# Compressed k and v projections of a sparse-attention layer: one pass over the contraction in place of two

## The chip, the core and the metric

One core of a Trainium2 chip runs the whole kernel. The metric is the device time of one execution in microseconds; lower is better. Several executions are timed and their median counts. Another execution is taken with a profiler, and the rows below come from that one.

## What is computed

One decoder layer on 256 positions of width 2048, in float32, with native sparse attention: three branches (compressed blocks, selected blocks, sliding window) with keys and values of their own. What matters here is the first step, the projections of the compressed branch and the compression behind them:

```python
h = x @ w_in                                   # x: 256 x 2048
q, kc, vc, ks, vs, kw, vw, gl, z = split_cols(h, NSA_SPLITS)   # kc, vc: 512 columns each
...
def nsa_compress(kv, pe, w1, w2):              # for kc and for vc
    blocks = kv[:, idx] + pe[None, None, :, None, :]           # 15 blocks of 32 positions, stride 16
    hid = silu(einsum('bnlgd,lde->bnge', blocks, w1))
    return einsum('bnge,ef->bngf', hid, w2)
```

Behind it come the other projections, the attention of 16 heads in four groups, a gate, the output projection and a layer norm.

## The kernel before

The contraction of 2048 is cut into 16 chunks of 128 (`KC`). Every float32 operand is split into an upper and a lower part: ScalarE writes the upper half (`whi`, `xs`; L66), VectorE subtracts to get the lower half (`wlo`; L67). `mm_w` (L102 to L104) then runs a pair of matmuls for one weight block of 128 columns and one chunk: the upper weights against both halves of x (512 columns), and the lower weights against the upper half of x (256 columns). The sum of both stands in one PSUM bank; `join` (L106 to L110) adds its two halves with one ScalarE and one VectorE instruction into one of two buffers.

The front of the program (L125 to L160) runs over "k", then over "v". Each has four column groups, so four PSUM banks: for k `proj` three times and `o`, for v `sc` twice and `tr` twice; these eight are all there are. In the k pass each step loads x (`load_x`, L78; four buffers `kt`) and the k weights (`big`, eight buffers, L134 to L137): one chunk at a time for the first eight, then two. The x halves stay in SBUF for all later projections. The v pass loads its weights in four loads of four chunks (`load_w`, L60, three buffers `wraw`). The weight splits go to `whi` and `wlo`, four buffers each. After its pass, each of k and v is joined and split into `hi` and `lo` of compressed layout (L154 to L159).

`compress_hidden` (L178) multiplies these with `w1`, 48 matmuls for each of k and v. Its weights come as two loads (`wraw`), split in four pieces (`whi`, `wlo`), one per twelve matmuls. It runs for k first; then come the table of the position bias (L232, L233) and the projections of group 0 (`proj_t`, L252), with the compression of v behind the first of them.

All loads are issued by SP in one queue. The program names the instructions in an order, and a scheduler sets the order on each engine from it, by a plan of the time at which buffers and operands come free. An instruction whose operands are there can go ahead of one named earlier.

Of the kernel before, what the change touches and what calls it, by code (L numbers as in the profile page):

```python
# [11 lines left out]
F32 = mybir.dt.float32  # L12
F32R = mybir.dt.float32r
# [3 lines left out]
P = 128  # L17
# [3 lines left out]
NG = 4  # L21
HPG = 4
KC = DM // P
NCMP = 15
CLEN = 32
CSTRIDE = 16
# [5 lines left out]
LU = 384  # L32
KTW = 4 * P + 16
CM = NG * 16 + 2
HALVES = ((0, 256), (256, 512))
HALF_TO = 1
CUTS_K = (0, 1, 2, 3, 4, 5, 6, 7, 8, 10, 12, 14, 16)


@with_exitstack  # L40
def nsa_layer(ctx, tc, A, out):
    nc = tc.nc
# [4 lines left out]
    wp = ctx.enter_context(tc.tile_pool(name="wp", bufs=1))  # L47
    sb = ctx.enter_context(tc.tile_pool(name="sb", bufs=1))
# [5 lines left out]
    def bank(tag):  # L54
        return ps.tile([P, 512], F32, name=tag, bufs=BUFS[tag])
# [4 lines left out]
    def load_w(src, k, n):  # L60
        raw = wp.tile([P, k, n], F32, name="wraw", bufs=3)
        nc.sync.dma_start(raw, src)
        return raw

    def split_into(hi, lo, src):
        act.activation(hi, src, AF.Copy)  # L66
        dve.tensor_tensor(lo, src, hi.bitcast(F32), op=ALU.subtract)  # L67

    def split_w(raw, k0, k1):
        n = raw.shape[2]  # L70
        hi = wp.tile([P, k1 - k0, n], F32R, name="whi", bufs=4)
        lo = wp.tile([P, k1 - k0, n], F32R, name="wlo", bufs=4)
        split_into(hi, lo, raw[:, k0:k1, :])
        return hi, lo
# [3 lines left out]
    def load_x(k0, k1):  # L78
        raw = sb.tile([P, KTW], F32, name="kt", bufs=4)[:, :(k1 - k0) * SEQ]
        raw = raw.rearrange("p (k s) -> p k s", s=SEQ)  # L80
        nc.sync.dma_start(raw, A["xT"][:, k0:k1, :])
        c, o = divmod(k0, 4)
        if o == 0:
            X2[c] = [xp.tile([P, 2, 2 * SEQ], F32R, name="xs") for _ in range(2)]
        t = X2[c][o // 2][:, o % 2:o % 2 + k1 - k0, :]
        hi, lo = t[:, :, :SEQ], t[:, :, SEQ:]
        if k0 == 0:
            dve.tensor_copy(hi, raw)
            dve.tensor_tensor(lo, raw, hi.bitcast(F32), op=ALU.subtract)
        else:  # L90
            split_into(hi, lo, raw)

    def xk(k):
        return X2[k // 4][k % 4 // 2][:, k % 2, :]

    def xh(k):
        return xk(k)[:, :SEQ]
# [4 lines left out]
    def mm_w(acc, hi, lo, k):  # L102
        pe.matmul(acc, hi, xk(k), start=(k == 0), stop=False)  # L103
        pe.matmul(acc[:, :SEQ], lo, xh(k), start=False, stop=(k == KC - 1))  # L104

    def join(acc, scale=1.0):  # L106
        t = sb.tile([P, SEQ], F32, name="join", bufs=2)
        act.activation(t, acc[:, SEQ:], AF.Copy, scale=scale)  # L108
        dve.scalar_tensor_tensor(t, acc[:, :SEQ], scale, t, op0=ALU.mult, op1=ALU.add)  # L109
        return t  # L110
# [4 lines left out]
    def load_small():  # L115
        for n, shape in (("peT_k", [P, CLEN]), ("peT_v", [P, CLEN]), ("w2_k", [P, P]), ("w2_v", [P, P]),
                         ("rel", [2 * CSTRIDE, NH]), ("gmask", [P, 3 * HPG])):
            t = const.tile(shape, F32, name=n)
            nc.sync.dma_start(t, A[n])
            small[n] = t  # L120
# [1 line left out]
    ident = const.tile([P, P], F32, name="ident")  # L122
    make_identity(nc, ident)

    tags = {"k": ["proj", "proj", "proj", "o"], "v": ["sc", "sc", "tr", "tr"]}  # L125
    kvc = {}
    cuts = {"k": CUTS_K, "v": (0, 4, 8, 12, 16)}
    for which, name in enumerate("kv"):
        accs = [bank(t) for t in tags[name]]
        for k0, k1 in zip(cuts[name], cuts[name][1:]):  # L130
            src = A["wkvc"][which, :, k0:k1, :]
            if name == "k":
                load_x(k0, k1)
                raw = sb.tile([P, CSTRIDE * CM], F32, name="big", bufs=8)[:, :(k1 - k0) * 512]  # L134
                raw = raw.rearrange("p (k n) -> p k n", n=512)
                for n0, n1 in HALVES if k0 < HALF_TO else ((0, 512),):
                    nc.sync.dma_start(raw[:, :, n0:n1], src[:, :, n0:n1])  # L137
            else:
                raw = load_w(src, k1 - k0, 4 * P)
            if name == "k" and k1 == KC:  # L140
                load_small()
            for ka in range(k0, k1, 2):
                kb = min(ka + 2, k1)
                if name == "k" and k0 < HALF_TO:
                    hi, lo = (wp.tile([P, 1, 512], F32R, name=n, bufs=4) for n in ("whi", "wlo"))
                    for n0, n1 in HALVES:
                        split_into(hi[:, :, n0:n1], lo[:, :, n0:n1], raw[:, :, n0:n1])
                else:
                    hi, lo = split_w(raw, ka - k0, kb - k0)
                for g in range(NG):  # L150
                    cs = slice(g * P, (g + 1) * P)
                    for k in range(ka, kb):
                        mm_w(accs[g], hi[:, k - ka, cs], lo[:, k - ka, cs], k)
        hi, lo = (sb.tile([P, CSTRIDE, CM], F32R, name="big", bufs=8) for _ in range(2))  # L154
        for g in range(NG):
            view = [t[:, :, g * 16:(g + 1) * 16].rearrange("p l n -> p n l") for t in (hi, lo)]
            split_into(*view, join(accs[g]).rearrange("p (n l) -> p n l", l=CSTRIDE))
        view = [t[:, :, 64:66].rearrange("p l a -> p a l") for t in (hi, lo)]
        split_into(*view, small["peT_" + name].rearrange("p (a l) -> p a l", a=2))  # L159
        kvc[name] = hi, lo  # L160
# [10 lines left out]
    for i in range(2):  # L171
        t = const.tile([P, HPG, 64], F32R, name=f"pcs{i}")
# [329 lines left out]
    def split_held(raw, half, hi):  # L502
        lo = sb.tile([P, 2, 512], F32R, name="bias", bufs=2)
        split_into(hi[:, 2 * half:2 * half + 2], lo, raw[:, 2 * half:2 * half + 2, :])
        return hi[:, 2 * half:2 * half + 2], lo

    for c in range(4):
# [4 lines left out]
        for hq in range(4):  # L512
            raw = load_w(A["wo"][c, hq], 4, 512)
            if c == 0 and hq == 3:
                load_res()
            for half in range(2):
                if c == 3 and hq == 1:
                    if half == 0:
                        held_hi = sb.tile([P, HPG, 512], F32R, name="t1", bufs=1)
                    w = split_held(raw, half, held_hi)  # L520
                else:
                    w = split_w(raw, 2 * half, 2 * half + 2)
# [19 lines left out]
        n0, n1 = Norm(0), Norm(1)  # L542
# [37 lines left out]
def _layout(inputs):  # L580
    f = lambda n: np.asarray(inputs[n])
    x = np.ascontiguousarray(f("x").reshape(SEQ, DM))
    w = f("w_in_a")

    def rows(a):
        return a.reshape(-1, P, a.shape[-1]).transpose(1, 0, 2)

    arr = {"x": x}
    arr["xT"] = rows(x.T)
    arr["wkvc"] = np.stack([rows(w[:, o:o + 512]) for o in (2048, 2560)])  # L590
    wt = []
    for g in range(NG):
        cols = [3072 + g * P, 4096 + g * P]
        cols += [(HPG * g + h) * P for h in range(HPG)]
        cols += [5168 + (HPG * g + h) * P for h in range(HPG)]
        wt += [rows(w[:, c:c + P]) for c in cols]
    arr["wt"] = np.stack(wt)
    wv = []
    for g in range(NG):
        panel = np.concatenate([w[:, 3584 + g * P:3584 + (g + 1) * P], w[:, 4608 + g * P:4608 + (g + 1) * P],  # L600
                                w[:, 5120 + 12 * g:5120 + 12 * (g + 1)]], axis=1)
        wv.append(np.stack([rows(panel[h * 1024:(h + 1) * 1024]) for h in range(2)]))
    arr["wv"] = np.stack(wv)
    wo = f("w_out_a")
    arr["wo"] = np.stack([np.stack([rows(wo[q * 512:(q + 1) * 512, c * 512:(c + 1) * 512]) for q in range(4)])
                          for c in range(4)])
    for n in "kv":
        arr["peT_" + n] = f("cmp_pe_" + n).T
        arr["w1_" + n] = f("cmp_w1_" + n).reshape(2, 16, P, P).transpose(2, 1, 0, 3).reshape(P, 16, 2 * P)
        arr["w2_" + n] = f("cmp_w2_" + n)  # L610
    arr["rel"] = f("rel_bias")
    arr["ln_g"] = f("ln_g_a")
    arr["ln_b"] = f("ln_b_a")
    oh = np.zeros((33, LU), np.float32)
    m = np.arange(LU)
    oh[_bucket(np.maximum(m - 127, 0)), m] = 1.0
    oh[:, :127] = 0.0
    oh[32, :127] = 1.0
    arr["onehot"] = oh
    cs = np.zeros((CM, 2, P), np.float32)  # L620
    for g in range(NG):
        for n in range(NCMP):
            j = 16 * g + n
            cs[j, 0, j] = cs[64, 0, j] = cs[j + 1, 1, j] = cs[65, 1, j] = 1.0
    arr["csel"] = cs
    gm = np.ones((P, HPG, 3), np.float32)
    gm[:31, :, 0] = 0.0
    arr["gmask"] = gm.reshape(P, 12)
    return {k: np.ascontiguousarray(v) for k, v in arr.items()}
# [15 lines left out]
```

## Time and profile before

| | us |
|---|---|
| median of 3 runs | 488.47 (487.57 to 489.68) |
| the profiled execution | 489.38 |
| its span, first to last instruction | 487.6 |
| TensorE busy in it | 471.4 (97%) |
| VectorE busy | 329.8 (68%) |
| ScalarE busy | 270.5 (55%) |

Busy time of an engine is the sum over its instructions, without overlaps. A releaser is the instruction or transfer that ended the idle time of an engine. Tiles are named as out<-in, and L103 is line 103 of the kernel.

### The profile page before, as it was taken

To read this page: it belongs to the slowest core of one execution; us is meant where nothing else is said; L and a number is where in the kernel's file an instruction comes from. 1 tells how busy PE (TensorE), PEld (TensorE's weight loads), DVE (VectorE), ACT (ScalarE), POOL (GpSimd) and SP (SyncE) were. 2 spreads that over 40 slices of the span, in tenths; PEclk is the share of its full clock that TensorE was granted. 3 is DMA by queue.
4 is the path that set the end of the run, shared out by engine and by line. 5 is a ranking of instruction groups with operands and counts; after the bars stand their busy time and mean duration, and the time that the engine had idled before them with its cause. 6 is when DMAs were issued, how large, how long until landed. Compare 5 with 4: busy or idle time off the path is not lost.

```text
span 487.6 us, 7526 instructions
## 1 busy us (share of the span) xinstructions
PE 471.4 (97%) x2804; PEld 416.3 (85%) x2804; DVE 329.8 (68%) x757; ACT 270.5 (55%) x540; POOL 11.3 (2%) x17
## 2 busy tenths in 40 slices
PE   6899999999999999999999999999999999999991
PEld 5788898899888889888889988888988888888890
DVE  5676875655878656777865686875677675576546
ACT  6565764547665645767555566655477544355410
POOL 1000000000000000000000000000000000000024
PEclk9999999999999999999999999999999999999996
DMA  8897597555453634263644444354427955276104
GB/s 257 275 358 257 183 319 281 177 173 174 173 173 129 214 140 173 93 250 105 224 159 173 172 161 134 140 187 167 173 89 257 403 173 192 97 245 223 49 12 162
DMA packets 19341, 91.37 MB, mean 187 GB/s; under 512 B 2422, under 2 KB 6633, under 8 KB 10089
## 3 DMA queue, kind: packets, MB, share of 16 engines
q1 hardware_dynamic: 19017, 90.63, 52.2%
q8 instruction: 22, 0.36, 0.3%
q10 hardware_dynamic: 288, 0.26, 0.2%
q14 instruction: 14, 0.11, 0.1%
HBM read 88.76 MB, written 2.12 MB: 186 GB/s over the span
## 4 chain that ended last, share of the span: by engine, by line
PE 94%; DMA 3%; DVE 2%; ACT 0%; SPq 0%; issue 0%; DVEq 0%; ACTq 0%
PE proj L103 31%; PE proj L104 16%; PE proj L455 3%; PE proj L454 3%; PE proj L453 3%; PE proj L298 3%; PE proj L297 3%; PE proj L296 3%; DMA big<-in_wkvc 3%; PE tr L391 2%; PE tr L103 2%; PE sc L453 2%; PE sc L455 2%; PE sc L103 2%; PE sc L454 2%; PE sc L344 1%
## 5 line engine op out<-in xcount | busy, mean ns | idle before, releaser
L103 PE MATMUL proj<-xs,whi 128*128 128x512 f32 x688 | 244.0, 398 | 5.3 <-ACT whi L66 5.3
L67 DVE TENSOR_TENSOR wlo<-wraw,whi 128x1024 fp32r<-128x1024 f32 (+1 forms) x142 | 174.2, 1229 | 105.7 <-ACT whi L66 102.6
L66 ACT ACTIVATE whi<-wraw 128x1024 fp32r<-128x1024 f32 (+1 forms) x142 | 150.7, 1063 | 133.2 <-PE proj L103 50.7
L104 PE MATMUL proj<-xs,wlo 128*128 128x256 f32 x688 | 190.1, 283 | 0.1
L103 PEld LDWEIGHTS proj<-xs,whi 128*128 128x128 f32 x688 | 128.7, 189 | 31.6 <-ACT whi L66 5.5
L104 PEld LDWEIGHTS proj<-xs,wlo 128*128 128x128 f32 x688 | 129.6, 189 | 3.1 <-DVE wlo L67 0.5
L354 ACT ACTIVATE t<-t,m 128x128 f32<-128x128 f32 (+3 forms) x96 | 37.6, 395 | 8.9 <-DVE m L352 8.8
L298 PE MATMUL proj<-wlo,xs 128*128 128x268 f32 x128 | 36.6, 286 | 0.0
L297 PE MATMUL proj<-whi,xs 128*128 128x268 f32 x128 | 36.5, 286 | 0.0
L296 PE MATMUL proj<-whi,xs 128*128 128x268 f32 x128 | 36.4, 285 | 0.0
L455 PE MATMUL proj<-whi,big 128*128 128x512 f32 (+1 forms) x76 | 28.6, 377 | 0.0
L454 PE MATMUL proj<-wlo,big 128*128 128x512 f32 (+1 forms) x76 | 28.6, 376 | 0.0
L453 PE MATMUL proj<-whi,big 128*128 128x512 f32 (+1 forms) x76 | 28.3, 376 | 0.0
L296 PEld LDWEIGHTS proj<-whi,xs 128*128 128x128 f32 x128 | 24.0, 188 | 0.4
L297 PEld LDWEIGHTS proj<-whi,xs 128*128 128x128 f32 x128 | 24.0, 188 | 0.1
L298 PEld LDWEIGHTS proj<-wlo,xs 128*128 128x128 f32 x128 | 24.1, 188 | 0.0
L394 ACT ACTIVATE ph<-tr 128x512 fp32r<-128x512 f32 x24 | 14.1, 598 | 15.9 <-PE tr L391 15.8
L109 DVE SCALAR_TENSOR_TENSOR join<-proj,join 128x256 f32<-128x256 f32 x43 | 17.9, 418 | 5.5 <-ACT join L108 5.5
L395 DVE TENSOR_TENSOR pl<-tr,ph 128x512 fp32r<-128x512 f32 x24 | 16.2, 687 | 6.0 <-ACT ph L394 5.5
L354 ACT ACTIVATION_READ_ACCUMULATOR t<-t,m 128x1 f32 x96 | 18.1, 189 | 0.0
L367 DVE TENSOR_SCALAR t<-t,coef 128x128 f32<-128x128 f32 (+1 forms) x64 | 17.8, 316 | 0.3
L352 DVE CUSTOM_DVE_ANT_0 t<-sc,bias 128x128 f32<-128x128 f32 (+2 forms) x80 | 17.3, 264 | 0.0
(153 smaller groups left out, 641.5 us busy)
## 6 DMA issues: line engine op xcount, KB each, us to landing
wraw<-in_wt SPq DMA_DIRECT2D x40, 1024.0 KB, 4.8
wraw<-in_wo SPq DMA_DIRECT2D x16, 1024.0 KB, 4.8
wraw<-in_wv SPq DMA_DIRECT2D x8, 1072.0 KB, 5.0
wraw<-in_wkvc SPq DMA_DIRECT2D x4, 1024.0 KB, 6.7
big<-in_wkvc SPq DMA_DIRECT2D x4, 512.0 KB, 8.8
wraw<-in_w_k SPq DMA_DIRECT2D x2, 1024.0 KB, 5.2
wraw<-in_w_v SPq DMA_DIRECT2D x2, 1024.0 KB, 5.0
bias<-u_dr SPq DMA_DIRECT2D x4, 512.0 KB, 7.5
```

The lines of the kernel that those rows point to most:

```text
L66: act.activation(hi, src, AF.Copy)
L67: dve.tensor_tensor(lo, src, hi.bitcast(F32), op=ALU.subtract)
L103: pe.matmul(acc, hi, xk(k), start=(k == 0), stop=False)
L104: pe.matmul(acc[:, :SEQ], lo, xh(k), start=False, stop=(k == KC - 1))
L109: dve.scalar_tensor_tensor(t, acc[:, :SEQ], scale, t, op0=ALU.mult, op1=ALU.add)
L296: pe.matmul(a, xh(k)[:, ts], hi[:, k4, :], start=(k == 0), stop=False)
L297: pe.matmul(a, xl(k)[:, ts], hi[:, k4, :], start=False, stop=False)
L298: pe.matmul(a, xh(k)[:, ts], lo[:, k4, :], start=False, stop=(k == KC - 1))
L354: act.activation(tt, tt, AF.Exp, bias=m[:, i:i + 1], scale=-1.0, accum_out=den[:, i:i + 1])
L453: pin(pe.matmul(y, ah, hi[:, h2, c0:c1], start=(hq == 0 and h == 0), stop=False))
L454: pin(pe.matmul(y, ah, lo[:, h2, c0:c1], start=False, stop=False))
L455: pin(pe.matmul(y, al, hi[:, h2, c0:c1], start=False, stop=(hq == 3 and h == 3)))
```

## The change

The two passes become one loop over the 16 chunks, with all eight banks open. The k and v weights lie side by side in memory (`wkvc` is 128 x 16 x 1024), and each chunk has one load of 512 KB into a `big` buffer and one split of 1024 columns. Chunk 0 is cut into 256, 256 and 512 columns. x is loaded for chunk 0, for chunk 1, and from then on for two chunks at a time. In a chunk the four k groups come first, then the four v groups; for chunks 13 to 15 (`LATE`) the v groups are held back until after the last k group. The joins and splits of k and v follow the loop.

```diff
-HALVES = ((0, 256), (256, 512))
-HALF_TO = 1
-CUTS_K = (0, 1, 2, 3, 4, 5, 6, 7, 8, 10, 12, 14, 16)
+FIRST = ((0, 256), (256, 512), (512, 1024))
+CUTS_X = (0, 1, 2, 4, 6, 8, 10, 12, 14, 16)
+LATE = 13
...
-    tags = {"k": ["proj", "proj", "proj", "o"], "v": ["sc", "sc", "tr", "tr"]}
+    tags = ["proj", "proj", "proj", "o", "sc", "sc", "tr", "tr"]
     kvc = {}
-    cuts = {"k": CUTS_K, "v": (0, 4, 8, 12, 16)}
+    accs = [bank(t) for t in tags]
+    late = []
+
+    def kv_mms(k, hi, lo, i0, i1):
+        for i in range(i0, i1):
+            cs = slice(i * P, (i + 1) * P)
+            mm_w(accs[i], hi[:, 0, cs], lo[:, 0, cs], k)
+
+    for k in range(KC):
+        if k in CUTS_X:
+            load_x(k, CUTS_X[CUTS_X.index(k) + 1])
+        raw = sb.tile([P, CSTRIDE * CM], F32, name="big", bufs=8)[:, :1024].rearrange("p (k n) -> p k n", k=1)
+        src = A["wkvc"][:, k:k + 1, :]
+        if k == 0:
+            hi, lo = (wp.tile([P, 1, 1024], F32R, name=n, bufs=4) for n in ("whi", "wlo"))
+            for n0, n1 in FIRST:
+                nc.sync.dma_start(raw[:, :, n0:n1], src[:, :, n0:n1])
+            for n0, n1 in FIRST:
+                split_into(hi[:, :, n0:n1], lo[:, :, n0:n1], raw[:, :, n0:n1])
+        else:
+            nc.sync.dma_start(raw, src)
+            hi, lo = split_w(raw, 0, 1)
+        if k == KC - 1:
+            load_small()
+        kv_mms(k, hi, lo, 0, NG)
+        if k < LATE:
+            kv_mms(k, hi, lo, NG, 2 * NG)
+        else:
+            late.append((k, hi, lo))
+    for args in late:
+        kv_mms(*args, NG, 2 * NG)
     for which, name in enumerate("kv"):
-        accs = [bank(t) for t in tags[name]]
-        for k0, k1 in zip(cuts[name], cuts[name][1:]):
-            src = A["wkvc"][which, :, k0:k1, :]
...
-                for g in range(NG):
-                    cs = slice(g * P, (g + 1) * P)
-                    for k in range(ka, kb):
-                        mm_w(accs[g], hi[:, k - ka, cs], lo[:, k - ka, cs], k)
         hi, lo = (sb.tile([P, CSTRIDE, CM], F32R, name="big", bufs=8) for _ in range(2))
         for g in range(NG):
             view = [t[:, :, g * 16:(g + 1) * 16].rearrange("p l n -> p n l") for t in (hi, lo)]
-            split_into(*view, join(accs[g]).rearrange("p (n l) -> p n l", l=CSTRIDE))
+            split_into(*view, join(accs[NG * which + g]).rearrange("p (n l) -> p n l", l=CSTRIDE))
...
-    arr["wkvc"] = np.stack([rows(w[:, o:o + 512]) for o in (2048, 2560)])
+    arr["wkvc"] = rows(w[:, 2048:3072])
```

## Rows read from the trace of the kernel before

**Rows 1.** The page: span, and busy time and instructions of TensorE.

```profile
span 487.6 us, 7526 instructions
PE 471.4 (97%) x2804; PEld 416.3 (85%) x2804; DVE 329.8 (68%) x757; ACT 270.5 (55%) x540; POOL 11.3 (2%) x17
```

**Rows 2.** Waits of TensorE in the whole span: us in total, times, longest.

```profile
PE proj L103 <- ACT whi L66: 5.3, 2, 3.9
```

**Rows 3.** Instructions in order of time, front: start, duration, engine, line, idle before.

```profile
3.88 1.65 PE L103 MATMUL proj<-xs,whi 128*128 128x512 f32 x3 [3.88 <-ACT whi L66]
10.37 0.86 PE L103 MATMUL proj<-xs,whi 128*128 128x512 f32 x3
53.12 0.28 PE L187 MATMUL proj<-whi,big 128*66 128x256 f32 x1
```

**Rows 4.** Busy time by stretch: length, PE, PEld, DVE, ACT, POOL, clock, DMA share, GB/s.

```profile
0.00:3.88 3.88, 0.00 (x1) 0.00 (x1) 1.04 (x6) 1.70 (x2) 1.66 (x9) 1.00 0.47 135
3.88:8.97 5.09, 5.09 (x17) 4.30 (x18) 3.15 (x7) 2.81 (x7) 0.00 (x0) 1.00 0.92 287
8.97:17.37 8.40, 8.40 (x50) 7.28 (x48) 5.64 (x11) 4.92 (x10) 0.00 (x0) 1.00 0.92 293
17.37:18.96 1.59, 0.16 (x2) 0.00 (x0) 0.02 (x1) 1.06 (x1) 0.00 (x0) 1.00 1.00 363
18.96:30.64 11.68, 11.61 (x64) 9.84 (x65) 8.00 (x10) 7.35 (x11) 0.00 (x0) 1.00 0.86 320
30.64:53.12 22.48, 22.48 (x131) 19.64 (x130) 15.86 (x21) 13.08 (x19) 0.00 (x0) 1.00 0.74 259
```

**Rows 5.** Instructions in order of time, ScalarE's split of the weights of chunks 8, 9.

```profile
17.86 1.06 ACT L66 ACTIVATE whi<-big 128x1024 fp32r<-128x1024 f32 x1 [2.11 <-DMA big<-in_wkvc]
```

**Rows 6.** SP's waits before issuing x (total, times, longest), and its issues in time.

```profile
SPq L81 <- DVE xs L67: 2.8, 6, 0.8
```

```profile
13.06 3.04 SPq L137 DMA_DIRECT2D big<-in_wkvc  x2
16.20 0.51 SPq L81 DMA_DIRECT2D kt<-in_xT  x1
```

**Rows 7.** Stretches of 2 us, columns as in rows 4; the last is GB/s.

```profile
12.00:14.00 2.00, 2.00 (x12) 1.72 (x11) 1.68 (x4) 1.37 (x3) 0.00 (x0) 1.00 0.78 202
14.00:16.00 2.00, 2.00 (x15) 1.78 (x14) 0.91 (x2) 0.82 (x2) 0.00 (x0) 1.00 0.85 243
```

**Rows 8.** Groups of instructions by shape: count, busy us, mean ns, idle before.

```profile
L66 ACT ACTIVATE whi<-wraw 128x1024 fp32r<-128x1024 f32 x16 | 16.9, 1059 | 9.9 <-PE tr L103 7.9 <-DMA wraw<-in_wkvc 1.1 <-PE proj L103 0.9
L66 ACT ACTIVATE big<-join 128x256 fp32r<-128x256 f32 x8 | 4.9, 699 | 0.3 <-DVE join L109 0.2
L108 ACT ACTIVATE join<-proj 128x256 f32<-128x256 f32 x3 | 1.0, 373 | 0.0
...
L67 DVE TENSOR_TENSOR wlo<-wraw,whi 128x1024 fp32r<-128x1024 f32 x16 | 19.3, 1221 | 10.2 <-ACT whi L66 7.4 <-PE proj L104 2.8
L67 DVE TENSOR_TENSOR big<-join,big 128x256 fp32r<-128x256 f32 x8 | 4.8, 646 | 0.0
L109 DVE SCALAR_TENSOR_TENSOR join<-proj,join 128x256 f32<-128x256 f32 x3 | 1.2, 415 | 0.0
...
L67 DVE TENSOR_TENSOR xs<-kt,xs 128x512 fp32r<-128x512 f32 x4 | 2.7, 684 | 0.9 <-ACT xs L66 0.9
L66 ACT ACTIVATE xs<-kt 128x512 fp32r<-128x512 f32 x4 | 2.5, 624 | 1.1 <-DMA kt<-in_xT 0.9
```

**Rows 9.** ScalarE in order of time around the end of the v pass.

```profile
51.37 0.36 ACT L108 ACTIVATE join<-sc 128x256 f32<-128x256 f32 x1
51.91 0.38 ACT L108 ACTIVATE join<-sc 128x256 f32<-128x256 f32 x1 [0.18 <-PE sc L104]
53.20 1.06 ACT L66 ACTIVATE whi<-wraw 128x1024 fp32r<-128x1024 f32 x1 [0.90 <-PE tr L103]
54.16 1.16 ACT L66 ACTIVATE big<-join 128x256 fp32r<-128x256 f32 x2
55.11 2.15 ACT L66 ACTIVATE whi<-wraw 128x1024 fp32r<-128x1024 f32 x2
```

**Rows 10.** TensorE in order of time: the bias-table matmul.

```profile
57.55 0.82 PE L233 MATMUL o<-ph,rel_aug 33*16 33x384 f32 x2
```

**Rows 11.** SP's issues in order of time behind the k pass.

```profile
25.45 0.53 SPq L164 DMA_DIRECT2D zth<-in_csel  x1
...
31.79 0.36 SPq L62 DMA_DIRECT2D wraw<-in_wkvc  x1
35.40 4.37 SPq L62 DMA_DIRECT2D wraw<-in_w_k  x2
```

More of the change, by code (lines that the diff above doesn't have):

```diff
@@ L123, in nsa_layer @@
     make_identity(nc, ident)
-    tags = {"k": ["proj", "proj", "proj", "o"], "v": ["sc", "sc", "tr", "tr"]}
+    tags = ["proj", "proj", "proj", "o", "sc", "sc", "tr", "tr"]
     kvc = {}
-    cuts = {"k": CUTS_K, "v": (0, 4, 8, 12, 16)}
-    for which, name in enumerate("kv"):
-        accs = [bank(t) for t in tags[name]]
-        for k0, k1 in zip(cuts[name], cuts[name][1:]):
-            src = A["wkvc"][which, :, k0:k1, :]
[L132 to L149, printed above, removed]
-                for g in range(NG):
-                    cs = slice(g * P, (g + 1) * P)
-                    for k in range(ka, kb):
-                        mm_w(accs[g], hi[:, k - ka, cs], lo[:, k - ka, cs], k)
```

## The prediction

> **What bounds the kernel now.** I read the page first: TensorE is busy 471.4 of 487.6 us [rows 1]. So time can be won only where TensorE stands still or runs below its pace. The waits of TensorE name just one releaser, ScalarE's split of weights, in two places that sum to 5.3 us [rows 2]; 3.88 us of it is the wait for the first weights [rows 3]. What does the rest cost? I cut the front into stretches [rows 4]. The undisturbed pace comes from the v pass: 64 pairs of matmuls (a 512-column one and its 256-column correction) in 22.48 us, 0.351 us per pair. The k and v passes are 128 pairs, 44.95 us at that pace, but they last from 3.88 to 53.12, 49.24 us. The missing 4.29 us lie as follows:
> - 3.88 to 8.97 (contraction chunks 0 and 1, eight pairs, 2.81 us at pace): 5.09 us, 2.28 lost. TensorE is busy throughout; its first matmuls simply last longer, though the granted clock reads 1.00 [rows 3, 4].
> - 8.97 to 17.37 (chunks 2 to 7, 24 pairs, 8.43 at pace): 8.40, nothing lost.
> - 17.37 to 18.96: 1.59 us with TensorE almost idle. ScalarE had waited 2.11 us for the weights of chunks 8 and 9 [rows 5].
> - 18.96 to 30.64 (chunks 8 to 15, 32 pairs, 11.24 at pace): 11.68, 0.44 lost.
>
> Why were those weights late? In the k pass a chunk needs 128 KB of x and 256 KB of weights, 393,216 bytes, in 4 x 0.351 = 1.405 us: 280 GB/s. The transfers brought 287 and 293 GB/s in the first two stretches [rows 4], so no lead is ever built. Then SP waits six times, 2.8 us in all, for a buffer of x to be split before it issues the next load; the last two weight loads and the x load behind them go out between 13.06 and 16.20 [rows 6], and the rate falls to 202 and 243 GB/s [rows 7]. After 30.64 the same TensorE work needs only weights and nothing waits.
>
> **The change: supply.** Both projections use a chunk of x while it is there. TensorE's work stays the same, 128 pairs; ScalarE and VectorE split the same number of weight columns. A chunk now carries 128 KB of x and 512 KB of weights, 655,360 bytes, but feeds eight pairs, 2.81 us: 233 GB/s, below the 287 to 293 that the same queue gave in this stretch. Does the start hold? By 3.88 us 0.52 MB had come, by 8.97 us 1.98 MB (135 and 287 GB/s) [rows 4]. The first matmul needs x of chunk 0 and 256 weight columns, as now, in the same order of issue, so it stays at 3.88. The slow start is a matter of time and not of chunks, as far as I can tell: I leave its 2.28 us, so that chunk 0 alone now fills the time to about 8.97. Chunk 1 is complete at 1.31 MB, about 6.6 us; with 1.06 us of ScalarE for its weights [rows 8] and a short split of x it is ready by 8.1. Chunk 2 with x for two chunks is complete at 2.10 MB, about 9.4 us, ready by 11.1 and wanted at 11.78. From there 655,360 bytes take 2.24 us at 293 GB/s against 2.81 us of matmuls, and the lead grows by 0.57 us per chunk. A dip to 202 GB/s would cost 0.43 us of lead per chunk; one of the length seen (4 us) is covered by the lead. ScalarE spends 1.06 us on a chunk's weights and half of 0.63 on x, VectorE 1.23 and half of 0.68 [rows 8], both under 2.81. Loads of x now carry two chunks from chunk 2 on, so ten issues replace twelve and SP waits less for x buffers. So the 1.59 and the 0.44 us should go: -2.03 us, with bounds of 1.5 (a first lead that is 0.5 us too short) and 2.03. The supply can win no more than this, since nothing else in the front is a wait.
>
> **The change: the turn from projection to compression.** This is where it can be lost. Now the four k banks are evacuated beside the v pass, whose 22 us hide everything. After the change k is finished by chunk 15, and only the v matmuls of chunks 13 to 15, twelve pairs, 4.21 us, are held back behind it. Call the last k matmul 0 and the end of the held-back ones 4.21; there the compression of k starts and needs all four k groups. Per group ScalarE does 0.37 + 0.70 us and VectorE 0.42 + 0.65 [rows 8], in turns, with two buffers of `join` between them. Laying these out by hand (first group ready at -1.05, since the four last k pairs end 0.35 apart) gives 4.1 us for the last upper half and 4.85 us for the last lower half: the first lower-half matmul, third in the compression, would wait some 0.6 us.
>
> Behind that stand the w1_k splits. They take four buffers of `whi`, which were last held by chunks 12 to 15. Now those buffers come free over the whole v pass; after the change the second to fourth come free at 1.40, 2.81 and 4.21, as the held-back v matmuls end, while ScalarE and VectorE are on the k groups. From -0.4 on VectorE owes 4.28 us for k, 1.23 per w1_k split and 4.28 for v. With k first and v last its second w1_k split ends at about 6.4 against a wanted 6.3 (4.21, the 0.6 wait and 12 matmuls): total stall 0.7 us. With two v groups drawn in between, as the scheduler draws them in now (two joins, a weight split, two group splits, two weight splits from 51.37 on) [rows 9], the second split is 0.5 us and the third 1.0 us late on top, and the stall is 2.3. I take 1.5, the middle, since the present order [rows 9] is such a mix. Against it stands the small bias-table matmul, which needs neither k nor w1 and runs for 0.82 us in the middle of the compression now [rows 10]: it can fill part of a stall that comes at 4.21. Net +0.7, from -0.1 to +2.3.
>
> **What is later.** w1_k and the first projection weights no longer wait for the v weights' buffers: now w1_k is issued at 35.40, after the fourth v load at 31.79 [rows 11]; after the change these buffers are empty from the start. What could that hurt? If they go out before the x and weights of chunks 9 to 15, 3.1 MB at the 320 to 363 GB/s of [rows 4] put about 9 us in front of them (a rival, below). The projections behind the compression have their weights at least 2 us early, and the added backlog on VectorE at 4.21 is 1 to 2.5 us, so I count nothing there.
>
> **Sum.** The profiled execution took 489.38 us, with 487.6 from first to last instruction and 1.78 outside. 489.38 - 2.03 + 0.7 = 488.05. The median of the three runs is 488.47, 0.91 below that execution, so the forecast on the median is 488.47 - 1.33, say 487.2.
>
> **Rivals.**
> (a) *The turn is fully hidden.* For it: the order is planned anew, so w1_k's first split can go long before, and the bias matmul can fill 0.8 us. Against it: the arithmetic above leaves 0.7 even in the best order. 488.47 - 2.03 = 486.4.
> (b) *Slower: all of v's evacuation goes ahead of the w1_k splits.* The program names v's joins before the compression. VectorE is then at work from -0.4 on k (4.28), v (4.28), with 0.8 of gaps for the ping-pong, and two w1_k splits (2.46): 11.4, and with v's banks not ready before 4.21, up to 12.2. The third quarter of the compression wants that at 7.0: 5.2 us of stall, 4.4 after the bias matmul. 488.47 - 2.03 + 4.4 = 490.9. It decides from a stall of more than 2.9 us (2.03 + 0.82). For it: no bank is free while all eight accumulate. Against it: now the scheduler mixes them [rows 9], and each v join waits for one of two buffers, which leaves room for a weight split.
> The Trainium skill (Perfetto Trace Analysis, Matmuls) asks that independent groups rotate through banks, so that one group's evacuation overlaps the next group's matmuls. The change gives this up for v, whose banks all close together at 4.21; by that rule (b) is the expected end, while rows 9 show v's banks evacuated behind their last matmul in the kernel before too, without a wait of TensorE.
> (c) *The loads are reordered.* SP's queue has w1_k and the first wt early; `csel` is issued at 25.45, before the fourth v load that stands ahead of it in the program [rows 11], so the order is not fixed. Issued after chunk 8, they delay chunk 9 from about 21 to 30 us, and it is wanted at 31.4 (8.97 + 8 x 2.81) less 1.1 for the split: on the edge. Issued four chunks earlier, 3 us of stall: 488.47 - 2.03 + 0.7 + 3 = 490.1; on average about 488.9.
> (d) *The late weights only move.* A stall like the 1.59 us comes at another chunk because the dip has a cause other than the x buffers: no gain, plus the turn, 489.0.
>
> **Chances.** Forecast 0.52, (a) 0.23, (b) 0.10, (c) 0.08, (d) 0.07. About 0.5%, 2.4 us, is what a measurement of this kernel tells from no change: faster means below 486.03, slower above 490.91. The forecast and (c), (d) lie inside. Of (a), 486.4 with a scatter like that of the three runs (487.57 to 489.68) falls below in some 0.09; of (b) and (c) some 0.06 lie above. So 0.09, 0.85, 0.06. The range: 486.2 (a, with a little scatter) to 489.4 (the net cost of 2.3 at the turn and a supply gain of 1.5 give 489.3).
>
> **What would show it.** Right: no gap of TensorE between 9 us and the end of the projections, these ending near 51; the releaser of the next wait is the split of `join` or of w1_k; the compression lasts longer than now by about 1.5 us less the bias matmul. Wrong: a wait for `in_wkvc` after chunk 1 (c, d); first matmuls slow for longer or shorter than to 8.97; a compression of k with no wait (a) or with over 3 us of it (b).

## The result and the profile after

The changed kernel takes 495.44 us (median of six runs, 493.85 to 495.74; the profiled execution 495.74); the kernel before takes 489.19 beside it (487.57 to 489.92). The ratio is 1.0127 (95% interval 1.0106 to 1.0148): 6.3 us slower, where the forecast was 487.2 in a range of 486.2 to 489.4. The page of the changed kernel, with a row of the granted clock in 40 slices:

```profile
span 493.9 us, 7507 instructions
...
PE 473.1 (96%) x2804; PEld 417.8 (85%) x2804; DVE 330.2 (67%) x751; ACT 270.2 (55%) x534; POOL 11.3 (2%) x17
...
PEclk9999799999999999999999999999999999999996
```

Against [rows 1] TensorE has the same 2,804 matmuls, busy for 1.7 us more, and stands still for longer. The clock row, never below 9 elsewhere except in the last slice, dips to 7 in its fifth slice. The waits of TensorE in the whole span (us in total, times, longest), to set beside [rows 2]:

```profile
PE proj L103 <- ACT whi L66: 4.7, 2, 3.9
PE o L238 <- DVE join L109: 4.7, 1, 4.7
```

The second line is new, and no rival named its releaser: VectorE's `join` of the fourth k bank (tag `o`). TensorE in order of time (start, duration, engine, line, idle before) shows where it lies:

```profile
10.19 0.97 PE L103 MATMUL proj<-xs,whi 128*128 128x512 f32 x3 [0.82 <-ACT whi L66]
...
49.44 0.85 PE L103 MATMUL proj<-xs,whi 128*128 128x512 f32 x3
...
50.81 0.62 PE L103 MATMUL tr<-xs,whi 128*128 128x512 f32 x2
51.27 0.52 PE L104 MATMUL proj<-xs,wlo 128*128 128x256 f32 x3
...
51.98 0.39 PE L104 MATMUL tr<-xs,wlo 128*128 128x256 f32 x2
57.03 1.46 PE L238 MATMUL o<-ph,rel_aug 33*16 33x384 f32 x2 [4.66 <-DVE join L109]
58.42 0.48 PE L192 MATMUL proj<-whi,big 128*66 128x256 f32 x1
...
65.37 0.39 PE L103 MATMUL proj<-xs,whi 128*128 128x512 f32 x1
...
482.16 0.28 PE L460 MATMUL proj<-whi,big 128*128 128x256 f32 x1
```

The four k banks are `proj` (three) and `o`, the v banks `sc` and `tr`. The last chunk runs as 512-column matmuls of k, then of v, then the corrections of k, then of v: the v matmuls of chunks 13 to 15 are not held back at all. The last correction of k comes half a microsecond before that of v, so all eight banks close within a microsecond, the last at about 52.2 (the second of the last two matmuls starts 0.12 behind the first, and 0.12 later a next one could start). ScalarE takes up a split of `w1_k` at 51.47 and begins on k at 52.44. The same two points of the kernel before, the first matmul behind the compression of k and the last one of all:

```profile
59.64 0.39 PE L103 MATMUL proj<-xs,whi 128*128 128x512 f32 x1
...
476.46 0.28 PE L455 MATMUL proj<-whi,big 128*128 128x256 f32 x1
```

From one to the other it takes 416.82 us before and 416.79 after: all but the tail of the difference is made in the front. Busy time by stretch of the changed kernel, columns as in [rows 4]:

```profile
3.88:9.20 5.32, 5.32 (x16) 4.44 (x16) 1.86 (x4) 1.47 (x4) 0.00 (x0) 1.00 0.90 274
9.20:10.19 0.99, 0.17 (x1) 0.00 (x0) 0.02 (x1) 0.99 (x2) 0.00 (x0) 1.00 0.98 333
10.19:51.00 40.81, 40.81 (x231) 35.68 (x232) 26.31 (x26) 21.89 (x25) 0.00 (x0) 1.00 0.77 291
56.00:60.00 4.00, 2.97 (x10) 1.71 (x11) 3.16 (x9) 3.34 (x8) 0.00 (x0) 0.50 0.50 203
```

The last row is new in kind: the granted clock is 0.50, the 1.2 GHz level. It fell while TensorE stood still, and the first 4.2 us of matmuls behind the wait, up to 61.2, run at it. The bias-table matmul lasts 1.39 us to its successor, against 0.75 before [rows 10], and the compression of k 6.95 against 5.77. So the 6.3 us between the two spans are:
- end of the projections, 52.2 against 53.12 [rows 3]: -0.9
- TensorE still until 57.03: +4.8
- bias matmul and compression, 57.03 to 65.37 against 53.12 to 59.64: +1.8 (8.34 less 6.52)
- behind the last matmul, 11.7 against 11.1: +0.6.

### The profile page after: what moved, and what is told of

Read it like the earlier page. It is cut to its first block, busy times and chain, and to the rows that moved or that the text cites. A ratio compares the mean times of both kernels' runs of the same rounds, so it can differ in the third digit from the quotient of the medians.

```text
span 493.9 us, 7507 instructions
## 1 busy us (share of the span) xinstructions
PE 473.1 (96%) x2804; PEld 417.8 (85%) x2804; DVE 330.2 (67%) x751; ACT 270.2 (55%) x534; POOL 11.3 (2%) x17
## 4 chain that ended last, share of the span: by engine, by line
PE 94%; DVE 2%; DMA 1%; ACT 1%; SPq 0%; issue 0%; DVEq 0%; ACTq 0%
PE proj L103 32%; PE proj L104 16%; PE proj L460 3%; PE proj L458 3%; PE proj L459 3%; PE proj L303 3%; PE proj L302 3%; PE proj L301 3%; PE tr L396 2%; PE sc L458 2%; PE sc L460 2%; PE sc L459 1%; PE tr L103 1%; PE sc L103 1%; DMA big<-in_wkvc 1%; PE sc L349 1%
## 5 line engine op out<-in xcount | busy, mean ns | idle before, releaser
L67 DVE TENSOR_TENSOR wlo<-wraw,whi 128x1024 fp32r<-128x1024 f32 (+1 forms) x134 | 164.5, 1229 | 101.2 <-ACT whi L66 101.0
L66 ACT ACTIVATE whi<-wraw 128x1024 fp32r<-128x1024 f32 (+1 forms) x134 | 142.3, 1064 | 126.9 <-PE proj L103 54.0
L67 DVE TENSOR_TENSOR wlo<-big,whi 128x1024 fp32r<-128x1024 f32 (+2 forms) x18 | 19.9, 1107 | 15.9 <-ACT whi L66 13.8
L66 ACT ACTIVATE whi<-big 128x1024 fp32r<-128x1024 f32 (+2 forms) x18 | 17.4, 966 | 19.1 <-DMA big<-in_wkvc 10.5
```

## The experiments

Ratios are to the kernel before, run beside. Three questions were open: does the lost hold-back make the wait; what does the clock cost; and what is left once both are mended?

**The hold-back, held on TensorE.** The matmuls of chunks 13 to 15 are kept in the order of the program; the loads stay as they are in the changed kernel.

```diff
-    def mm_w(acc, hi, lo, k):
-        pe.matmul(acc, hi, xk(k), start=(k == 0), stop=False)
-        pe.matmul(acc[:, :SEQ], lo, xh(k), start=False, stop=(k == KC - 1))
+    def mm_w(acc, hi, lo, k, pin=lambda i: i):
+        pin(pe.matmul(acc, hi, xk(k), start=(k == 0), stop=False))
+        pin(pe.matmul(acc[:, :SEQ], lo, xh(k), start=False, stop=(k == KC - 1)))
...
+            mm_w(accs[i], hi[:, 0, cs], lo[:, 0, cs], k, keep if k >= LATE else lambda i: i)
```

> The changed kernel, with the matmuls of chunks 13 to 15 held in the order in which the program names them: k of 13, 14, 15, then v of 13, 14, 15. Nothing else is held; w1_k still goes out ahead of the last four weight loads. Theory A (the wait of 4.7 us behind the projections is there because the plan undid the hold-back, so that the four k banks close together with the v banks and their joins and splits lie bare): k closes 4.2 us before v, at about 48.1; the k groups are ready at about 53 to 54; the wait behind the projections falls from 4.7 us to 1 to 2 us, the granted clock stays at 1.00 there, the compression of k ends near 60 in place of 65.4, and the time is 489.5 to 490.5. Rival B (the plan mixed the chunks because the weights of chunks 14 and 15 do arrive late behind w1_k): a wait for in_wkvc before k of chunk 14 or 15 takes the place, 2 us or more, and the time stays above 493.

Measured: 492.43 (490.65 to 494.05, nine runs), ratio 1.0059 (1.0039 to 1.008). TensorE at the turn, and its busy time behind it:

```profile
51.63 0.80 PE L238 MATMUL o<-ph,rel_aug 33*16 33x384 f32 x2 [0.16 <-PE tr L104]
53.23 0.34 PE L192 MATMUL proj<-whi,big 128*66 128x256 f32 x1 [0.79 <-ACT big L66]
...
54.95 0.34 PE L194 MATMUL proj<-whi,big 128*66 128x256 f32 x1 [1.27 <-DVE big L67]
```

```profile
56.00:60.00 4.00, 4.00 (x26) 4.00 (x25) 3.35 (x6) 3.66 (x7) 0.00 (x0) 0.67 0.94 321
```

The 4.8 us wait is gone and 3.0 us come back; waits of 0.8 and 1.3 us remain, for the split k groups. The clock still dips (0.67 from 56 to 60). The loads of `w1_k` and of the first projection weights stand ahead of the last two weight chunks here too, and TensorE does not wait for a chunk behind the second one. The time is above the 489.5 to 490.5 that I expected: the waits are as long as expected or a little longer, and I had not expected the clock to fall.

**The loads, held in the order of the program.** Nothing is said to the scheduler about matmuls; only SP's loads of x, `wkvc`, the small inputs, `csel`, the first two `w1_k` loads and `onehot` are kept in order.

```diff
-            nc.sync.dma_start(raw, src)
+            keep(nc.sync.dma_start(raw, src))
...
-        nc.sync.dma_start(raw, A["xT"][:, k0:k1, :])
+        keep(nc.sync.dma_start(raw, A["xT"][:, k0:k1, :]))
```

> The changed kernel, with SP's loads held in program order up to w1_k; the matmuls are not held. The plan then leaves the v matmuls of chunks 13 to 15 behind k by itself. Theory A (w1_k and the first projection weights, 3 MB drawn ahead of the last four weight loads in the plan, made the plan drop the hold-back): as with the matmuls held, the wait behind the projections is 1 to 2 us, the compression of k ends near 60, the time is 489.5 to 490.5, and the weights of chunk 14 are split by 36 rather than at 40.6. Rival B (w1_k is then late itself, since it is issued behind all weights): a wait of the compression for w1_k, the time above 491.

Measured: 492.55 (490.44 to 494.31, ten runs), ratio 1.0058 (1.0039 to 1.0077). With the loads in order the hold-back came by itself: the k matmuls of chunk 15 end at 47.7, the held-back v matmuls at 51.9. So it was the order of the loads that cost the changed kernel its hold-back. SP's issues in the changed kernel:

```profile
25.17 0.91 SPq L62 DMA_DIRECT2D wraw<-in_w_k  x2
...
27.78 0.33 SPq L62 DMA_DIRECT2D wraw<-in_wt  x1
28.21 1.11 SPq L147 DMA_DIRECT2D big<-in_wkvc  x2
```

Three megabytes of weights for the stages behind the turn stand ahead of the weights of the last chunks. On the chip this does little: ScalarE waits 3.41 us for `in_wkvc` ahead of the split at 40.55, TensorE not at all there. But the order of all engines is laid down before the run. A plan in which the last chunks are late has no k work to put ahead of the held-back v matmuls; that this is how the scheduler came to its order is my reading, the plan's own times were not seen. Built with `LATE` at 16, no hold-back at all (not run), the program has the same order of instructions on every engine as with 13: in the changed kernel the hold-back is a line of the program without an effect.

Why does a kernel that does hold back still wait? TensorE and ScalarE of this run:

```profile
53.78 0.33 PE L196 MATMUL proj<-whi,big 128*66 128x256 f32 x1 [0.78 <-ACT big L70]
...
55.50 0.33 PE L198 MATMUL proj<-whi,big 128*66 128x256 f32 x1 [1.27 <-DVE big L71]
```

```profile
49.45 1.05 ACT L70 ACTIVATE whi<-wraw 128x1024 fp32r<-128x1024 f32 x1
...
51.12 2.03 ACT L70 ACTIVATE whi<-wraw 128x1024 fp32r<-128x1024 f32 x2
53.03 0.69 ACT L70 ACTIVATE big<-join 128x256 fp32r<-128x256 f32 x1
```

Three splits of `w1_k` (3.1 us) stand ahead of the split of the last k group, the one that the first matmul wants.

Of these two kernels, the matmuls or the loads held, the 19 executions differ by their mean granted clock. Seven at 0.991 took 490.4 to 491.6; twelve at 0.985 to 0.988 took 492.3 to 494.3. So with the hold-back restored and the clock up, the kernel is still about 2 us above the kernel before, and in most executions the clock costs about 2 us more. The time that I expected, 489.5 to 490.5, was missed here too.

**The clock by itself.** The changed kernel, with its wait filled: 22 matmuls with a weight of zeros add nothing to the last v bank while VectorE works on k.

```diff
+    zero = const.tile([P, P], F32R, name="zero")
+    pool.memset(zero.bitcast(F32), 0.0)
...
+    for i in range(NFILL):
+        keep(pe.matmul(accs[7], zero, xk(0), start=False, stop=(i == NFILL - 1)))
```

> The changed kernel with 22 more matmuls of 512 columns with zero weights into the last v bank, behind the last v matmul: about 4.8 us of TensorE work laid into the wait of 4.7 us. They add zeros. Theory A (part of the loss is the lower granted clock behind the wait: 0.50 in 56 to 60, the bias table takes 1.39 us in place of 0.75 and the compression of k 6.95 in place of some 5.7): the clock stays at 1.00, the bias table starts at 57 as now, the compression of k ends at 63.5 in place of 65.4, and the time is about 1.8 us less than that of the changed kernel, 493.6. Rival B (the compression is slow because it waits for its own splits): no change, 495.4, or later by what the added matmuls overrun.

Measured: 493.73 (493.6 to 494.02, four runs), ratio 1.0084 (1.0061 to 1.0106).

```profile
52.01 5.28 PE L162 MATMUL tr<-xs,zero 128*128 128x512 f32 x22
57.23 0.81 PE L243 MATMUL o<-ph,rel_aug 33*16 33x384 f32 x2
```

```profile
56.00:60.00 4.00, 4.00 (x24) 2.72 (x23) 3.10 (x8) 3.48 (x9) 0.00 (x0) 1.00 0.45 188
```

The bias matmul starts 0.2 later than in the changed kernel, so the evacuation is no sooner. But the clock stays at 1.00, and from there to the end of the compression it takes 6.53 us (to 63.76) instead of 8.34. The 1.8 us in the account above are the clock's; the median falls by 1.7.

**Less held back.** On top of the ordered loads, v is held back for two chunks instead of three.

```diff
-LATE = 13
+LATE = 14
```

> The kernel with SP's loads in program order (sporder), with LATE = 14: only the v matmuls of chunks 14 and 15 are held back, 2.8 us in place of 4.2. Theory A (what the turn costs is the k joins and splits that the held-back matmuls don't cover): the waits behind the last v matmul grow by about 1.4 us over the 2.2 us of sporder, to 3.5, and with a longer gap the granted clock falls below 1.00 in most executions: 494 to 495. Rival B (the turn is bound by something else, such as w1_k): the same waits and time as sporder, 492.5.

Measured: 493.91 (493.37 to 494.52, four runs), ratio 1.0092 (1.0059 to 1.0124), 1.4 us above the three chunks. The wait ahead of the bias matmul is back, and the clock from 56 to 60 is 0.50. The waits at the turn sum to 2.6 us, against 2.2 with three chunks and the 3.5 that I expected; the rest of the 1.4 us I put down to the clock, 0.985 to 0.988 in all four executions.

```profile
53.62 0.80 PE L242 MATMUL o<-ph,rel_aug 33*16 33x384 f32 x2 [1.57 <-issue]
...
55.80 0.48 PE L198 MATMUL proj<-whi,big 128*66 128x256 f32 x1 [1.00 <-DVE big L71]
```

The time follows the length of the hold-back: 495.4 with none (and the loads of the changed kernel), 493.9 with two chunks, 492.5 with three.

**More buffers for `join`.** On top of the ordered loads, four buffers instead of two, so that ScalarE can empty all four k banks without waiting for VectorE.

```diff
-        t = sb.tile([P, SEQ], F32, name="join", bufs=2)
+        t = sb.tile([P, SEQ], F32, name="join", bufs=4)
```

> sporder, with four buffers of join in place of two. ScalarE's order in the plan then has one w1_k split ahead of the last k group in place of three. Theory A (the 2.2 us of waits at the turn are the w1_k splits, 1.06 us each on ScalarE, drawn in between the k groups while these wait for a join buffer): the wait for the last k group falls to 0 to 0.8 us, the clock stays at 1.00, and the time is 490.3 to 491. Rival B (the k groups themselves are too slow for 4.2 us of cover: 4.3 us of VectorE work): the wait stays at 1.3 us or more, time above 491.5.

Measured: 489.12 (487.96 to 489.63, ten runs), ratio 0.9996 (0.9979 to 1.0014), 3.4 us below the same kernel with two buffers, more than I had put on it. ScalarE and TensorE at the turn:

```profile
49.89 1.08 ACT L70 ACTIVATE whi<-wraw 128x1024 fp32r<-128x1024 f32 x1
50.86 0.70 ACT L70 ACTIVATE big<-join 128x256 fp32r<-128x256 f32 x1
```

```profile
52.25 0.82 PE L242 MATMUL o<-ph,rel_aug 33*16 33x384 f32 x2
```

One `w1_k` split instead of three precedes the last k group, TensorE does not wait at the turn, and all ten executions have a clock of 0.990 or more. The compression of k ends at 58.69, 2.3 us sooner than with two buffers (60.95); the two profiled executions, both without a fall of the clock behind the start, differ by 2.1 us (489.18 and 491.29). The rest of the 3.4 I put down to the clock, which no longer falls in any execution.

**The late chunk 1.** On top of the ordered loads, the weights of chunk 1 are loaded and split in two halves, so that k can start on the first.

```diff
+PARTS = {0: FIRST, 1: ((0, 512), (512, 1024))}
...
-        if k == 0:
+        if k in PARTS:
```

> sporder, with the weights of chunk 1 in two loads and splits of 512 columns, k first. Theory A (the wait of about 0.9 us before chunk 1 is there because a load of 512 KB lands only when its last part is in, with the loads behind it sharing the queue): k of chunk 1 lands earlier, the wait before chunk 1 falls from 0.9 to under 0.3 us, and the projections end 0.6 to 0.9 us earlier; time 0.5 to 0.9 us under sporder's 492.5. Rival B (the bytes up to there are simply not in, at 250 to 290 GB/s): the wait stays at 0.7 us or more.

Measured: 492.74 (491.83 to 493.89, six runs), ratio 1.0074 (1.0049 to 1.0098). TensorE in the front:

```profile
8.42 0.86 PE L108 MATMUL proj<-xs,whi 128*128 128x512 f32 x3
...
9.88 0.73 PE L108 MATMUL sc<-xs,whi 128*128 128x512 f32 x2 [0.37 <-ACT whi L71]
...
12.21 0.96 PE L108 MATMUL proj<-xs,whi 128*128 128x512 f32 x3 [0.22 <-ACT whi L71]
```

Chunk 1 starts at 8.42, where the kernel with ordered loads has it at 9.84 and the changed kernel at 10.19. But most of these 1.4 us are not the load's: the wait before chunk 1 was only 0.31 us with ordered loads, and chunk 0 itself ends 1.1 us sooner here (8.42 against 9.53), since its matmuls become fast at 7.49 and not at 9.22 (the last experiment comes back to this). Two short waits follow, and the bias matmul comes at 51.76 instead of 52.19. In the time nothing of it is seen: all six executions have a clock of 0.985 to 0.989, and this scatter is larger than the 0.4 us. The run is inconclusive.

**Both.** Four `join` buffers and the split chunk 1, on the ordered loads (the two edits above).

> The changed kernel with loads in program order, four join buffers, and the weights of chunk 1 in two loads: what cost time at the turn and at chunk 1 mended, the one pass kept. Theory A (the one-pass form then gives what the supply promised, no more than the kernel before with x in pairs): the wait before chunk 1 is under 0.6 us in all, no wait at the turn over 0.4 us, time 488.3 to 489.0. Rival B (chunk 1 in two loads only moves the wait to chunk 2): as sp_join4, 489.1 or more.

Measured: 488.88 (487.41 to 489.91, twelve runs), ratio 0.9984 (0.9967 to 1.0). TensorE, and ScalarE behind the compression:

```profile
51.05 0.82 PE L243 MATMUL o<-ph,rel_aug 33*16 33x384 f32 x2
...
70.74 0.38 PE L109 MATMUL proj<-xs,wlo 128*128 128x256 f32 x1 [0.77 <-DVE wlo L72]
```

```profile
68.36 2.01 ACT L71 ACTIVATE whi<-wraw 128x1024 fp32r<-128x1024 f32 x2 [3.26 <-DMA wraw<-in_wt]
```

The projections end at 51.05, 2.07 us before those of the kernel before, and the compression of k at 57.49, 2.15 sooner: the front gains what the forecast had hoped for. It does not stay. ScalarE waits 3.26 us for projection weights, TensorE 0.77 at 70.74 behind it, and the last matmul starts at 475.68, only 0.8 us sooner than before (476.46). The whole loss lies at this place: matmul by matmul, the lead over the kernel before is 2.2 us up to 68.75 and 0.8 from 76.9 on.

**And a longer hold-back.** The same with v held back for four chunks (`LATE = 12`).

> sporder with all three: chunk 1 in two loads, four join buffers, and LATE = 12, that is 5.6 us of v matmuls held back. Theory A (start and turn are all that the one-pass form costs): no wait of TensorE over 0.4 us between 3.88 and the end of the compression of k, this ends near 58 against 59.64 in the kernel before, and the time is 487 to 488, below the 489.2 of the kernel before and the 488.6 of the kernel before with x in pairs. Rival B (what is taken from the turn comes back later, as ScalarE and VectorE carry k, v and w1_k at once): a new wait in the compressions or the first projections of group 0, time 488.8 or more.

Measured: 489.68 (488.96 to 490.69, twelve runs), ratio 1.0011 (0.9997 to 1.0026). A missed expectation: the scheduler again puts splits of `w1_k` among those of the k groups, and the compression waits 0.7 us. More hold-back was not better here.

**The reason of the supply.** I had laid the stall of the kernel before at chunk 8 to the buffers of x. This is the kernel before with only its loads of x in fewer, larger pieces; both passes stay.

```diff
+CUTS_X = (0, 1, 2, 4, 6, 8, 10, 12, 14, 16)
...
-                load_x(k0, k1)
+                if k0 in CUTS_X:
+                    load_x(k0, CUTS_X[CUTS_X.index(k0) + 1])
```

> The kernel before, with x loaded for two chunks at a time from chunk 2 on, as the change does it; the two passes stay. Theory A (the 1.59 us at 17.4 us came from waits for x buffers before issues of SP): the six waits of SP, 2.8 us, go, the stall of TensorE at chunk 8 goes, and the time is 1.5 to 2 us below the kernel before, ratio 0.996 to 0.997. Rival B (the supply is too slow by itself at 280 GB/s wanted, and the buffers only mark it): a stall of 1 to 2 us remains at some chunk from 2 to 15 and the ratio is 0.999 to 1.003.

Measured: 488.59 (488.14 to 489.19, twelve runs), ratio 0.9985 (0.9973 to 0.9998). Waits of TensorE, and a stretch that holds the dip of [rows 7]:

```profile
PE proj L104 <- ACT whi L67: 3.9, 1, 3.9
```

```profile
12.00:17.00 5.00, 5.00 (x31) 4.37 (x30) 3.44 (x6) 3.82 (x6) 0.00 (x0) 1.00 1.04 412
```

SP's waits for x buffers and the stall at chunk 8 are gone, and the queue brings 412 GB/s where it brought 202 and 243. So the loads of x made the stall. Whether by their buffers or by their size no run separates, as the edit changes both. The compression of k ends at 58.10 instead of 59.64, and the last matmul starts at 474.92 instead of 476.46: the 1.5 us stay to the end of TensorE's work. The profiled span gains 1.0 and the median 0.6, less than I expected. The difference to the span lies behind the last matmul, 11.7 us here against 11.1.

**The slow start.** On top of that, five matmuls of zeros into a bank that is not yet in use run while the first weights come.

```diff
+    zero = sb.tile([P, 512], F32R, name="ph", bufs=2)
+    dve.memset(zero.bitcast(F32), 0.0)
+    warm = bank("tr")
+    for i in range(NWARM):
+        pe.matmul(warm, zero[:, :P], zero, start=(i == 0), stop=(i == NWARM - 1))
```

> The kernel before with x in pairs (before_x2), with five matmuls of 512 columns on zeros ahead of the first projection, from about 1.4 us on, while TensorE waits for the first weights. Theory A (the slow first matmuls, 2.28 us lost to 8.97, are a matter of time since TensorE began to work, as the prediction assumed and as chunk 0 alone filled the same stretch in the changed kernel): the full pace comes 1.5 to 2.4 us earlier, the projections end 0.8 to 1.3 us earlier than in before_x2, and the time is 487.3 to 487.8. Rival B (the first matmuls are slow because of their own operands, which arrive late): no change, 488.6.

Measured: 488.49 (488.02 to 488.92, twelve runs), ratio 0.9978 (0.9965 to 0.9991).

```profile
1.46 2.50 PE L128 MATMUL tr<-ph 128*128 128x512 f32 x5 [1.46 <-DVE ph L125]
3.88 1.62 PE L105 MATMUL proj<-xs,whi 128*128 128x512 f32 x3
...
7.54 0.40 PE L105 MATMUL o<-xs,whi 128*128 128x512 f32 x1
...
8.94 0.93 PE L105 MATMUL proj<-xs,whi 128*128 128x512 f32 x3 [0.53 <-DVE xs L69]
```

The first matmuls are as slow as before; full pace (0.40 us) is there by 7.54, where the kernel before still took 0.63 at 7.88. Then x of chunk 2 is not there, and half a microsecond of the gain is a wait. The compression ends 0.46 us sooner than without the zeros; the expected time was lower, and the two medians, from two sittings, can't be told apart.

What are the slow matmuls? Here are two corrections of 256 columns in the kernel before, and a matmul of 256 columns in the changed kernel at a granted clock of 0.50:

```profile
6.39 0.41 PE L104 MATMUL o<-xs,wlo 128*128 128x256 f32 x1
...
8.85 0.28 PE L104 MATMUL o<-xs,wlo 128*128 128x256 f32 x1
```

```profile
58.91 0.42 PE L194 MATMUL proj<-whi,big 128*66 128x256 f32 x1
```

The slow ones have the length of the 1.2 GHz level. The 1.00 of [rows 4] for this stretch is no reading: the trace's list of granted clocks has its first entry at 8.72 us in the kernel before and at 10.05 in the changed one, with 1.00, and time without an entry is shown as 1.00. In the kernel before the matmuls become fast at that very entry.

Did the zeros bring it forward? That is not shown. The entry comes between 7.2 and 10.4 us in the twelve profiles. With the zeros it is earliest, at 7.16, but three kernels without them (the matmuls held, the filled wait, the late chunk 1) have it at 7.46 to 7.53, and the changed kernel, which begins just as the first two of these, has it at 10.05. One profile of each can't tell an effect of 1 or 2 us from this scatter.

These last two kernels are the only ones with an interval wholly below 1, by 0.2%.

## Why the prediction was wrong

By its own sum, on the profiled execution, the span was to be 488.05 - 1.78 = 486.3; it is 493.9. The 7.6 us between them, step by step:

**The turn: +0.7 forecast, 6.6 measured (4.8 of wait and 1.8 of clock). This is the step that failed,** at the sentence "After the change k is finished by chunk 15, and only the v matmuls of chunks 13 to 15, twelve pairs, 4.21 us, are held back behind it". I read that from the program and laid out ScalarE and VectorE from it, though the same text said of rival (c) that "the order is not fixed" on SP's queue, and [rows 9] showed that it isn't on ScalarE's. The hold-back was a request that the scheduler did not grant. That the change doesn't do what it says should have been a rival, with a price from the rows at hand: four k groups on ScalarE and VectorE, and TensorE with nothing to do. The groups of 0.37 + 0.70 and 0.42 + 0.65 us [rows 8], in turns over two `join` buffers, came to 4.1 and 4.85 us in my layout, the upper and the lower halves. VectorE of the changed kernel at the turn:

```profile
52.56 1.23 DVE L67 TENSOR_TENSOR wlo<-wraw,whi 128x1024 fp32r<-128x1024 f32 x1 [1.55 <-ACT whi L66]
53.70 0.75 DVE L109 SCALAR_TENSOR_TENSOR join<-proj,join 128x256 f32<-128x256 f32 x2
...
57.19 1.18 DVE L67 TENSOR_TENSOR big<-join,big 128x256 fp32r<-128x256 f32 x2 [0.21 <-ACT big L66]
```

The lower halves are done at 58.4, 6.2 us behind 52.2: the 4.85 with a `w1_k` split ahead of them, which ends at 53.7. The bias matmul was named as the one that waits because it stands first in the queue and takes the fourth k bank; it fills the last 1.4 us of this.

**With the hold-back granted the layout fell short too.** I had the turn at +0.7 net, from -0.1 to +2.3. With ordered loads and two `join` buffers, at full clock, it takes 9.1 us from the end of the projections to the end of the compression (51.9 to 60.95), against 6.5 in the kernel before (53.12 to 59.64): +2.6. That this lies near the upper end is luck. I had all k groups ahead of the `w1_k` splits, and put the upper end down to these being late behind groups of v. In the run it is the other way round: three `w1_k` splits, 3.1 us, stand ahead of the last k group, and the compression waits for that. With four buffers it takes 6.5 us (52.2 to 58.69), which is net 0: the turn hidden, as rival (a) had it for two buffers.

**Rival (b)**, 4.4 us of wait net, came closest in size but not in cause: not v's evacuation ahead of `w1_k` but k's own, which no matmul covered. The rule of the Trainium skill that stood beside it (Perfetto Trace Analysis, Matmuls: rotate groups through banks so that the evacuation of one lies beside the matmuls of another) speaks of this, and the trace agrees: eight banks that close within a microsecond cost a wait of 4.8 us, against 2.05 (0.78 + 1.27) for the same work with the v matmuls behind k's.

**Rival (c)** came true in its condition, `w1_k` and `wt` ahead of the last weights, though behind chunk 12 and not behind chunk 8, and its price came another way: nothing by late weights (the first experiment has that order and no wait of TensorE for them), everything through the order of the matmuls.

**The clock** was in no step. A wait at the turn was priced at its length, and 1.8 us of slower matmuls behind it were left out, which makes a wait of 4.8 us one of 6.6.

**Supply: -2.03 forecast, -0.9 measured,** the mechanism right, the first lead mis-sized. The stall at chunk 8 is gone, with nine loads of x in place of twelve (the prediction counts ten), and the queue gave 416 and 420 GB/s from 12 to 16, more than I had allowed. But chunk 1 was to be "complete at 1.31 MB, about 6.6 us". ScalarE's split of it:

```profile
9.08 1.06 ACT L66 ACTIVATE whi<-big 128x1024 fp32r<-128x1024 f32 x1 [2.95 <-DMA big<-in_wkvc]
```

It landed at 9.08, 2.5 us later, when 0.50 + 1.42 = 1.9 MB had come (128 and 274 GB/s, windows of the changed kernel): bytes of the loads behind it arrive before its own last ones. Cumulative bytes say when a load can be complete at the earliest, not when it is. Chunk 1 began at 10.19 instead of 8.97, and this 1.2 is the shortfall: a wait at another chunk, as in rival (d), but not from the dip. With chunk 1 in two loads and the hold-back in force the projections did end 2.07 us sooner. The slow start was a matter of time and not of chunks: chunk 0 alone filled 3.88 to 9.20, where two chunks had filled 3.88 to 8.97. But the prediction took its 1.00 for a reading and its 2.28 us for a constant. It is the lower clock, and its end varies from profile to profile: chunk 0 ended at 8.4 in the kernels with the filled wait and with the late chunk 1.

**What is late next,** where I counted nothing, was not reached by the changed kernel, and failed where the front was mended: of 2.15 us won, 0.8 were left behind the wait for projection weights at 70.74.

**The tail.** 0.6 us lie behind the last matmul. The engines' work there takes 8.2 us before and after; the rest is the write of the output. The profiles of all kernels here have 11.1 to 11.9 us there, with that of the kernel before at the low end, so this part is no effect of the change that I could show.

Open: how the scheduler came to its order in the changed kernel; and why the clock falls in some executions of a kernel and not in others with the same waits of 0.8 and 1.3 us. The kernel before has such executions too. Its only wait behind the first is the 1.4 us at chunk 8, and of its 76 executions timed beside the experiments ten have a clock of 0.988 or 0.989 and take 490.9 to 491.8. Of the 24 executions of the two kernels without this wait (x in larger pieces, with and without zeros) none has. That the wait is the cause is not shown.

## What to carry to other kernels

An order that the program states is a wish where a scheduler lays out the engines: before costing a hold-back, price the case in which it is not granted, and look for what could make the scheduler's picture differ from the chip's, such as loads whose buffers have come free early. Eight open PSUM banks save a pass over the inputs, and make the turn behind it the place that decides: it needs matmuls behind the first group, and enough staging buffers for all banks of that group. A large edit that removes a stall is best weighed against the smallest one that does: fewer, larger loads of x alone gave 0.6 us, no less than the best one-pass form here (0.4).

## What the runs showed of the hardware that I had not expected

- TensorE's granted clock fell to 0.50 within a single wait of 4.8 us and stayed there for the first 4.2 us of matmuls behind it (0.42 us for a 256-column one instead of 0.28), costing 1.8 us; filled with zeros the same stretch kept 1.00. With waits of 0.8 and 1.3 us, 0.45 us apart, twelve of 19 executions have a lower mean clock and take about 2 us longer; one of them is profiled, and its clock falls right behind these waits.
- At the start the matmuls run at the pace of the lower clock (0.63 us against 0.40 for 512 columns). The profile shows 1.00 there only because its record of the clock begins later, between 7.2 and 10.4 us in these twelve profiles.
- A 512 KB load issued at 3.06 landed at 9.08 with 0.6 MB more in by then than it and all ahead of it needed.
